# Seven block products instead of eight in the up projection of a hybrid decoder layer, with the projections around it regrouped

## The chip, the cores and the metric

The kernel runs on one core of one Trainium2 chip. Times are device microseconds (us) of one execution. The engines are PE (TensorE, matrix products; it accumulates in PSUM banks), DVE (VectorE), ACT (ScalarE), POOL (GpSimd) and SP (SyncE, which here only issues DMAs). Each engine works through its own queue in order; waits between engines go by semaphores.

## What is computed

One layer of a decoder for 576 tokens: 512 tokens of one prompt and 64 of samples (8 sequences of 8). A mixing part (a pooling branch, a recurrent branch and an attention over memory, joined by gates) gives `merged`; the change begins behind it. Of the reference that is:

```python
h = h + merged @ lw['w_out']                                   # 1024 -> 1024
xn2 = rmsnorm(h, lw['g_ffn'])
gv = xn2 @ lw['w_up']                                          # 1024 -> 2 x 3072
g_pre, val = gv[..., :D_FF], gv[..., D_FF:]
g_conv, new_ffn = causal_dwconv(g_pre, ffn_buf, lw['ffn_conv_w'], lw['ffn_conv_b'])   # 3 taps along the tokens
h = h + (jax.nn.gelu(g_conv) * val) @ lw['w_down']             # 3072 -> 1024
```

Behind it stand a last norm and the output. All is float32.

## The kernel before

Activations lie transposed: 128 features on the partitions, the 576 tokens along a row. A matrix product of float32 is made as three products of a shorter float type: weights and activations are split into a high part `wh`, `xh` (a cast on ACT, L97) and a low part `wl`, `xl` (the rest, a subtraction on DVE, L98), and PE does wh·xh, wh·xl and wl·xh for each 128 features of the inner dimension (`mm3`, L175; `wmm`, L191). A product of one 128-wide output tile with 1024 inner features is 3 x 8 x 2 = 48 matmuls, two token halves of 288 columns (`H288`) each into a PSUM bank of its own; the gate half of the up projection cuts 256 + 320 instead.

Weights stream. A class `Weights` (L113) loads each 128x1024 tile (512 KB) by a DMA on SP's queue into one of two raw buffers, two tiles ahead, and splits it into one of three pairs of high and low buffers.

Stages behind the mixing part, in the order of the program:

- `op_msplit(m)` splits the eight tiles of `merged`. The last tile is summed last (L491, DVE) after the last branch product.
- `op_out(m)` (L725), m = 0 to 7: 48 matmuls, residual add (L728), split of the normed-to-be tile, squares for the norm.
- `op_rstd_h` (L739): the sum of squares through PE (L225), a square root and Newton steps on ACT and DVE (`rs_`, `rt_`, `rv_`), and back over all partitions through PE (L249). The first tile's product is issued ahead of it.
- For each of 24 tiles j of the 3072: `op_up_g_mm`/`op_up_g` (gate: evacuation times the norm L271/L274, state copy L752, convolution L755/L757, gelu L761/L762, the value's norm L763 on POOL) and `op_up_v_mm`/`op_up_v` (value: product L774 and its split). After each eight tiles, `op_down(gr, m)` (L777) multiplies these eight into all eight output tiles; the third group runs as `op_down_last(c, m)` (L784) in token halves 320 and 256 with the last norm between (`op_fin_cols`, `op_final`, L820) and the stores (L821).

The order of issue is written out by hand (a string `MIX` and a rule in `make_schedule`); a scheduler then orders each engine's queue by it.

## Time and profile before

| | us |
|---|---|
| median of 3 runs | 975.23 (974.44 to 977.73) |
| profiled execution, its span | 974.6 |
| mixing part, up to the first product of the output projection | 447.1 |
| output projection | 51.2 |
| one tile j of the up projection | 12.8 |
| one group of `op_down` | 51.2 |

The profile gives for each engine its busy time and share of the span, the clock that was granted to TensorE, and the chain of work that ended last. The chain in order of time lists, from the end of the program back to its start, the work that released what came next; a long block of one engine without others between means that this engine set the time there. Windows give each engine's busy time in a stretch; groups by line give the mean duration of one instruction of a shape.

### The profile page before, as it was taken

How to read it: one execution, taken by the hardware profiler on the slowest of the kernel's cores; microseconds unless marked ns; L12 is line 12 of the kernel's file. 1: busy time of each engine (PE TensorE's matmuls, PEld its weight loads, DVE VectorE, ACT ScalarE, POOL GpSimd, SP SyncE). 2: the span in 40 equal slices, each digit the busy share in tenths (PEclk: the TensorE clock that was granted, in tenths of full speed). 3: DMA queues.
4: the chain of work that ended last, by engine and by line, in shares of the span. 5: the costliest groups of instructions: out<-in, count | busy, mean ns of one | idle time of the engine just before them, and what ended most of it. 6: DMA issues, size and time to landing. Idle time of an engine off the chain costs nothing.

```text
span 974.6 us, 17085 instructions
## 1 busy us (share of the span) xinstructions
PE 954.4 (98%) x7196; PEld 940.9 (97%) x7196; DVE 534.9 (55%) x768; ACT 389.3 (40%) x579; POOL 198.8 (20%) x265
## 2 busy tenths in 40 slices
...
PEclk9999999999999999999999999999999999999998
...
GB/s 227 136 77 66 77 72 70 102 159 113 77 108 131 150 198 149 142 109 88 87 87 65 87 87 88 84 69 87 87 87 85 71 84 87 87 86 71 132 156 118
DMA packets 33612, 101.00 MB, mean 104 GB/s; under 512 B 3936, under 2 KB 8032, under 8 KB 33536
## 3 DMA queue, kind: packets, MB, share of 16 engines
...
q8 instruction: 56, 0.92, 0.4%
q10 hardware_dynamic: 1088, 1.18, 0.3%
...
## 4 chain that ended last, share of the span: by engine, by line
PE 92%; DVE 4%; DMA 2%; ACT 1%; issue 1%; SPq 0%; POOL 0%; DVEq 0%; ACTq 0%
PE ps_up_g_mm L183 16%; PE ps_up_v_mm L183 16%; PE ps_gate L183 14%; PE ps_down L183 11%; PE ps_branch L183 10%; PE pq_down_last L183 5%; PE ps_out L183 5%; PE ps_rnn_mm L183 3%; PE ps_q L183 3%; PE ps_pool_mm L183 2%; PE pq_rnn_gate L183 1%; PE pq_k_mm L183 1%; PE ps_v L542 1%; DMA cv_spv<-in_cv 1%; DMA wr_start<-in_w_gate 1%
## 5 line engine op out<-in xcount | busy, mean ns | idle before, releaser
L183 PE MATMUL ps_up_g_mm<-y_out,wh_up_g_mm 128*128 128x256 f32 (+1 forms) x672 | 117.3, 297 | 0.0
L183 PE MATMUL ps_up_v_mm<-y_out,wh_up_v_mm 128*128 128x288 f32 x672 | 116.8, 296 | 0.0
L183 PEld LDWEIGHTS ps_up_g_mm<-y_out,wh_up_g_mm 128*128 128x128 f32 x672 | 101.3, 190 | 0.1
L183 PEld LDWEIGHTS ps_up_v_mm<-y_out,wh_up_v_mm 128*128 128x128 f32 x672 | 99.1, 189 | 0.0
L752 POOL COPY so_ffn<-e_up_g_mm 128x18 f32<-128x18 f32 x24 | 28.4, 1182 | 262.3 <-DVE e_up_g_mm L274 262.3
L183 PE MATMUL ps_up_g_mm<-y_out,wl_up_g_mm 128*128 128x256 f32 x336 | 72.2, 297 | 0.0
L183 PE MATMUL ps_up_v_mm<-y_out,wl_up_v_mm 128*128 128x288 f32 x336 | 72.0, 296 | 0.0
L97 ACT ACTIVATE wh_up_v_mm<-wr_up_v_mm 128x1024 fp32r<-128x1024 f32 x24 | 25.5, 1061 | 103.9 <-PE ps_up_g_mm L183 96.6
L183 PE MATMUL ps_down<-x_up_v,wh_down 128*128 128x288 f32 x384 | 66.7, 296 | 0.0
L271 DVE TENSOR_TENSOR e_up_g_mm<-ps_up_g_mm,s_rstd_h 128x512 f32<-128x512 f32 x24 | 16.6, 692 | 81.1 <-PE ps_up_g_mm L183 78.6
L183 PE MATMUL ps_gate<-x_start,wh_gate 128*128 128x288 f32 x320 | 57.0, 298 | 0.0
L183 PEld LDWEIGHTS ps_up_g_mm<-y_out,wl_up_g_mm 128*128 128x128 f32 x336 | 56.7, 190 | 0.0
L183 PEld LDWEIGHTS ps_down<-x_up_v,wh_down 128*128 128x128 f32 x384 | 56.5, 189 | 0.0
L183 PEld LDWEIGHTS ps_up_v_mm<-y_out,wl_up_v_mm 128*128 128x128 f32 x336 | 54.1, 189 | 0.0
L780 DVE TENSOR_TENSOR h<-ps_down,h 128x576 f32<-128x576 f32 x16 | 12.1, 757 | 68.0 <-PE ps_down L183 68.0
L183 PEld LDWEIGHTS ps_gate<-x_start,wh_gate 128*128 128x128 f32 x320 | 47.2, 189 | 1.0 <-issue 1.0
L761 ACT ACTIVATE g_up_g<-e_up_g 128x512 f32<-128x512 f32 x24 | 15.2, 634 | 80.2 <-DVE e_up_g L757 80.2
L97 ACT ACTIVATE wh_branch<-wr_branch 128x1024 fp32r<-128x1024 f32 (+1 forms) x24 | 22.0, 917 | 63.1 <-PE ps_gate L183 28.1
L774 DVE TENSOR_TENSOR g_up_g<-ps_up_v_mm,g_up_g 128x576 f32<-128x576 f32 x24 | 18.1, 756 | 52.6 <-POOL g_up_g L763 52.6
L97 ACT ACTIVATE wh_down<-wr_down 128x1024 fp32r<-128x1024 f32 x16 | 16.9, 1059 | 74.8 <-PE ps_down L183 72.7
L763 POOL TENSOR_TENSOR g_up_g<-g_up_g,s_rstd_h 128x576 f32<-128x576 f32 x24 | 34.6, 1443 | 58.9 <-ACT g_up_g L762 58.9
L183 PE MATMUL pq_down_last<-x_up_v,wh_down_last 128*128 128x256 f32 (+1 forms) x224 | 44.6, 295 | 0.1
...
## 6 DMA issues: line engine op xcount, KB each, us to landing
wr_up_g_mm<-in_w_up SPq DMA_DIRECT2D x21, 512.0 KB, 3.4
wr_up_v_mm<-in_w_up SPq DMA_DIRECT2D x21, 512.0 KB, 3.4
wr_down_last<-in_w_down SPq DMA_DIRECT2D x14, 512.0 KB, 3.5
wr_down<-in_w_down SPq DMA_DIRECT2D x12, 512.0 KB, 3.4
wr_gate<-in_w_gate SPq DMA_DIRECT2D x10, 512.0 KB, 3.5
ck_sscore<-in_ck SPq DMA_DIRECT2D x8, 512.0 KB, 4.4
cv_spv<-in_cv SPq DMA_DIRECT2D x8, 512.0 KB, 4.7
wr_branch<-in_w_gate SPq DMA_DIRECT2D x6, 512.0 KB, 3.7
```

The costliest lines, as they stand in the source:

```text
L97: nc.scalar.activation(hi, src, AF.Copy)
L183: nc.tensor.matmul(out[:, c, : hs.stop - hs.start], a[:, ks], b[:, hs], start=(first and k == 0 and i == 0), stop=(last and k == K - 1 and ...
L271: nc.vector.tensor_tensor(v2(ext[:, off : off + NP_]), p_[:, :, :256], v2(rbt[:, :NP_]), ALU.mult)
L542: nc.tensor.matmul(vps[:, mt, :], a[:, ms], b[:, ws], start=(k == 0 and i == 0), stop=(k == 7 and i == 2))
L752: nc.gpsimd.tensor_copy(so_ffn[:, j], sview(ext, 512, 10, 9)[:, :, 0:2])
L761: nc.scalar.activation(ge[:, :NP_], gc[:, :NP_], AF.Gelu_apprx_tanh)
L763: eng(OPT["gemul"]).tensor_tensor(ge, ge, rf, ALU.mult)
L774: nc.vector.tensor_tensor(v2(ge), p_[:, :, :TH], v2(ge), ALU.mult)
L780: nc.vector.tensor_tensor(v2(h[m]), p_[:, :, :TH], v2(h[m]), ALU.add)
```

## The change

The two factors of the up projection are cut in two: the 1024 inner features into halves K1 and K2 (four 128-wide tiles each), the output tiles of one j into gate and value, the tokens into two halves of 288. That makes a 2x2 block product, with 8 block products of 12 matmuls of 288 columns. The new code forms sums and differences of blocks and needs seven (Strassen's scheme in Winograd's form): `P1` to `P7`, 84 matmuls for a tile pair j where there were 96.

With it come:

- The normed activations are wanted in seven operand forms: `B11`, `B21`, `B22` (three of the four quarters), `T1`, `T2`, `T3`, `T4` (sums and differences). Each is made once, 1152 columns wide (four tiles of 288), by DVE additions, an ACT cast and a DVE subtraction.
- The norm is now applied to the activations themselves, in token halves (`norm`, L836), so the sum of squares is done once per token half, and the output projection runs in two token passes (`out_mm`, 24 matmuls of 288 columns for each half and tile). Five of the eight weight tiles of w_out stay in buffers between the passes (`wo_load`).
- The weight blocks are combined for each j: `R` holds two blocks and a third (768 KB, two DMAs of SP), `S` is the sum of two blocks; the second is added by a DMA that POOL issues (`accum_op`, L856). DVE adds two more (L873, L887). Five splits follow: two of 1024 columns (`prep_A`, `prep_S`) and three of 512.
- Products are combined behind PE: two PSUM banks take two block products each, three partial sums go through SBUF (`u`, `u3`, `v`): copies on ACT (L913, L919), sums on DVE (L925, L931, L941/L942, L950, L968). The first tap of the convolution moves to ACT (L957), the product with the value to POOL (L974).
- `w_down` works in six groups of four tiles; from j = 4 on, two output tiles of the group before (24 matmuls each) follow each j. The last group runs as before in columns 320 and 256 (`last_mm`, 12 matmuls), from weights kept in the form buffers. The first norm's multiplies (`final(0)`) now stand before the last product of the second columns.
- The first four j run ahead without down products: `P1` and `P2` of j = 0 to 3 stand in front, between the forms, and each of these j then has `P6`, `P7`, `P5`, `P4`, `P3`.

Matmuls from the output projection on: before 384 + 2304 + 1152 = 3840, after 384 + 2016 + 1152 = 3552.

```diff
     def op_msplit(m):
-        S["mg", m] = split(merged[m], T, tx)
-
...
+        for c, tag in enumerate(("xa", "xb")):
+            if (c, m // 2) not in mgh:
+                mgh[c, m // 2] = xu(tag, [2, 2, TH])
+            t = mgh[c, m // 2][:, m % 2]
+            split_to(t[:, 0], t[:, 1], merged[m][:, H288[c]])
...
+        def out_mm(c, m):
+            p_ = bank()
+            wh, wl = wo[m]
             for k in range(8):
...
+                x = mgh[c, k // 2][:, k % 2]
+                ks = slice(k * P, (k + 1) * P)
+                for i, (a, b) in enumerate(((wh, 0), (wh, 1), (wl, 0))):
+                    nc.tensor.matmul(
+                        p_[:, :TH], a[:, ks], x[:, b], start=(k == 0 and i == 0), stop=(k == 7 and i == 2)
+                    )
+            return p_
...
+        def out_post(c, m, p_):
+            hs = h[m][:, H288[c]]
+            nc.vector.tensor_tensor(hs, p_[:, :TH], hs, ALU.add)
+            s = tu()
+            nc.scalar.activation(s, hs, AF.Square)
...
+            nc.scalar.activation(hw[c][m // 4][:, m % 4, :], hs, AF.Identity, scale=pc(C_GFFN + m))
...
+        def load_R(j):
+            R[j] = fr.tile([P, 1536], F32, tag="R", name=nm("R"))
+            nc.sync.dma_start(R[j][:, 512:], w2(wu[j][:, 2:4]))
+            nc.sync.dma_start(R[j][:, :512], wu[j][:, 0])
+
+        def load_S(j):
+            SR[j] = raw()
+            nc.sync.dma_start(SR[j], w2(wu[j][:, 0:2]))
+            nc.gpsimd.dma_start(SR[j], w2(wu[j][:, 1:3]), accum_op=ALU.add)
...
+        def prep_A(j):
+            WA[j] = ring()
+            r = R.pop(("A", j)) if ("A", j) in R else R[j][:, 512:]
+            split_to(*WA[j], r)
+
+        def prep_S2(j):
+            r = R[j]
+            nc.vector.tensor_tensor(r[:, 512:1024], r[:, 512:1024], SR[j][:, :512], ALU.add)
+            W1[j, 6] = single()
+            split_to(*W1[j, 6], r[:, 512:1024])
+
+        def prep_S(j):
+            WS[j] = ring()
+            split_to(*WS[j], SR[j])
+
+        def prep_22(j):
+            W1[j, 4] = single()
+            split_to(*W1[j, 4], R[j][:, :512])
+
+        def prep_S4(j):
+            r = R[j]
+            nc.vector.tensor_tensor(r[:, 1024:], r[:, 1024:], r[:, 512:1024], ALU.add)
+            W1[j, 3] = single()
+            split_to(*W1[j, 3], r[:, 1024:])
...
+        def prod(p_, w, c0, x, first=True):
+            wh, wl = w
+            xh, xl = B[x]
+            for k in range(4):
+                ks = slice(c0 + k * P, c0 + (k + 1) * P)
+                for i, (a, b) in enumerate(((wh, xh), (wh, xl), (wl, xh))):
+                    nc.tensor.matmul(
+                        p_[:, :TH], a[:, ks], b[:, k, :],
+                        start=(first and k == 0 and i == 0), stop=(k == 3 and i == 2),
+                        skip_group_check=not first,
+                    )
+
+        C = {}
...
+        def P1(j):
+            C["b1", j] = bank()
+            prod(C["b1", j], WA[j], 0, "B11")
+            C["u", j] = tu()
+            nc.scalar.activation(C["u", j], C["b1", j][:, :TH], AF.Copy)
+
+        def P2(j):
+            p_ = C.pop(("b1", j))
+            prod(p_, WA.pop(j), 512, "B21", first=False)
+            C["v", j] = te(T)
+            nc.scalar.activation(C["v", j][:, :TH], p_[:, :TH], AF.Copy)
+
+        def P6(j):
+            p_ = bank()
+            prod(p_, W1.pop((j, 6)), 0, "T2")
+            u = C["u", j]
+            nc.vector.tensor_tensor(u, p_[:, :TH], u, ALU.subtract)
+
+        def P7(j):
+            C["b7", j] = p_ = bank()
+            prod(p_, WS[j], 512, "T3")
+            C["u3", j] = tu()
+            nc.vector.tensor_tensor(C["u3", j], p_[:, :TH], C["u", j], ALU.add)
+
+        def P5(j):
+            C["b5", j] = p_ = bank()
+            prod(p_, WS.pop(j), 0, "T1")
+            u3 = C.pop(("u3", j))
+            C["x", j] = ext = FF["x"].tile([P, UW], F32, tag="x", name=nm("ext"))
...
+        def P4(j):
+            p_ = C.pop(("b7", j))
+            prod(p_, W1.pop((j, 4)), 0, "T4", first=False)
+            ext = C["x", j]
+            nc.vector.tensor_tensor(ext[:, 2 : 2 + TH], p_[:, :TH], C["u", j], ALU.add)
...
+        def conv(j):
+            ext = C["x", j]
...
+            nc.scalar.activation(gc[:, :592], ext[:, 0:592], AF.Identity, scale=pc(cw), bias=pc(C_FCB + j))
+            for q_ in range(1, 3):
+                nc.vector.scalar_tensor_tensor(
+                    gc[:, :592], ext[:, q_ : q_ + 592], pc(cw + q_), gc[:, :592], ALU.mult, ALU.add
+                )
+            nc.scalar.activation(ext[:, :NP_], gc[:, :NP_], AF.Gelu_apprx_tanh)
+            nc.scalar.activation(sview(ext, NP_, 8), sview(gc, 512, 10)[:, :, 2:10], AF.Gelu_apprx_tanh)
...
+        def P3(j):
+            p_ = C.pop(("b5", j))
+            prod(p_, W1.pop((j, 3)), 0, "B22", first=False)
+            nc.vector.tensor_tensor(C["v", j][:, TH:], p_[:, :TH], C.pop(("u", j)), ALU.subtract)
+
+        prods = {}
+
+        def post(j):
+            v, ext = C.pop(("v", j)), C.pop(("x", j))
+            nc.gpsimd.tensor_tensor(v, v, ext[:, :T], ALU.mult)
+            t = xu(("xa", "xb")[j % 2], [2, T])
+            prods[j] = t[:, 0], t[:, 1]
+            split_to(t[:, 0], t[:, 1], v)
...
+        P1(0)
+        r2 = rstd_cols(sqs[1], TH)
+        P1(1)
+        prep_A(3)
+        rl2 = bcast(r2)
+        norm(1, 0, rl2)
+        norm(1, 1, rl2)
+        P2(0)
+        x11, x21 = hw[0]
+        x12, x22 = hw[1]
+        nc.vector.tensor_tensor(x11, x11, x12, ALU.subtract)
+        xt2 = xu("xa", [4, TH], F32)
+        nc.vector.tensor_tensor(xt2, x22, x11, ALU.add)
+        form("T2", 0, xt2)
+        P2(1)
+        nc.vector.tensor_tensor(x12, x12, x22, ALU.subtract)
+        prep_S(0)
+        load_S(1)
+        form("T3", 1, x12)
+        P1(2)
+        form("T1", 2, x11)
+        P1(3)
+        nc.vector.tensor_tensor(x21, x21, xt2, ALU.subtract)
+        prep_22(0)
+        form("T4", 3, x21)
+        P2(2)
+        form("B22", 4, x22)
+        prep_S4(0)
+        load_R(2)
+        P2(3)
+        hrs.close()
+        FF["x"] = pool("fx", 4)
+
...
+            n = j + 1
+            more = n < NFF
+            npre = n < NPRE
+            if not pre:
+                P1(j)
+                if more:
+                    prep_A(n)
+            P6(j)
+            if more and pre and not npre:
+                prep_A(n)
+            if more:
+                prep_S2(n)
+            if not pre:
+                P2(j)
+            P7(j)
+            P5(j)
+            if more:
+                prep_S(n)
+                if n + 1 < NFF:
+                    load_S(n + 1)
+            P4(j)
+            conv(j)
+            if more:
+                prep_22(n)
+            P3(j)
+            if more:
+                prep_S4(n)
+                if n + 2 < NFF:
+                    load_R(n + 2)
+            post(j)
+            if not pre:
+                down(g, 2 * q)
+            if more and not npre:
+                load_D(n // NFB - 1, n % NFB)
+                prep_D(n // NFB - 1, n % NFB)
+            if not pre:
+                down(g, 2 * q + 1)
...
+    def up_blocks(w):
+        b = w.reshape(2, 4, P, 2, NFF, P).transpose(4, 2, 3, 0, 1, 5)
+        return C(np.stack([b[:, :, 0, 1], b[:, :, 0, 0], b[:, :, 1, 0], b[:, :, 1, 1]], 2).reshape(NFF, P, 4, 512))
```

How the queues of DVE change is seen at three places. The first is the end of the mixing part, from the split of the last branch weight to the first residual add. Before:

```order
L98 TENSOR_TENSOR wl_branch_7_4973<-wr_branch_7_4970,wh_branch_7_4972 128x1024
L98 TENSOR_TENSOR x_msplit_5019<-g_gate_4_1487,x_msplit_5018 128x576
L487 TENSOR_TENSOR y_gate_7_4929<-ps_branch_7_4976,y_gate_7_4929 128x576
L98 TENSOR_TENSOR wl_out_5030<-wr_out_5027,wh_out_5029 128x1024
L491 TENSOR_TENSOR g_gate_7_1848<-g_gate_7_1848,y_gate_7_4929 128x576
L98 TENSOR_TENSOR x_msplit_5024<-g_gate_7_1848,x_msplit_5023 128x576
L728 TENSOR_TENSOR h<-ps_out_5033,h 128x576
```

After (`xa`, `xb` are the two token halves of a split merged tile):

```order
L112 TENSOR_TENSOR wl_branch_7_4975<-wr_branch_7_4972,wh_branch_7_4974 128x1024
L112 TENSOR_TENSOR xa_msplit_5016<-g_gate_4_1485,xa_msplit_5016 128x288
L112 TENSOR_TENSOR xb_msplit_5019<-g_gate_4_1485,xb_msplit_5019 128x288
L502 TENSOR_TENSOR y_gate_7_4929<-ps_branch_7_4978,y_gate_7_4929 128x576
L112 TENSOR_TENSOR wl_ffn<-wr_ffn,wh_ffn 128x1024
L506 TENSOR_TENSOR g_gate_7_1846<-g_gate_7_1846,y_gate_7_4929 128x576
L112 TENSOR_TENSOR xa_msplit_5009<-g_gate_7_1846,xa_msplit_5009 128x288
L112 TENSOR_TENSOR xb_msplit_5012<-g_gate_7_1846,xb_msplit_5012 128x288
L813 TENSOR_TENSOR h<-pb_ffn,h 128x288
```

The last merged tile (`g_gate_7`) is still summed behind the split of a weight; its own split is now two operations of 288, and the first residual add has 288 columns.

The second place is the start of the up stage. Before, DVE has there the norm's small operations, two weight splits and the first evacuations:

```order
L98 TENSOR_TENSOR wl_up_v_mm_5591<-wr_up_v_mm_5588,wh_up_v_mm_5590 128x1024
L229 TENSOR_SCALAR rv_rstd_h<-pq_rstd_h 128x4
L232 TENSOR_SCALAR rv_rstd_h<-pq_rstd_h 64x1
L98 TENSOR_TENSOR wl_up_g_mm_5692<-wr_up_g_mm_5689,wh_up_g_mm_5691 128x1024
L234 RECIPROCAL rs_rstd_h<-rt_rstd_h 128x8
L235 TENSOR_TENSOR rt_rstd_h<-rs_rstd_h 128x8
L236 SCALAR_TENSOR_TENSOR rt_rstd_h<-rt_rstd_h,rv_rstd_h 128x8
L237 SCALAR_TENSOR_TENSOR rs_rstd_h<-rt_rstd_h,rs_rstd_h 128x8
L271 TENSOR_TENSOR e_up_g_mm_5530<-ps_up_g_mm_5539,s_rstd_h 128x512
L274 TENSOR_TENSOR e_up_g_mm_5530<-ps_up_g_mm_5539,s_rstd_h 128x8x8
L755 TENSOR_SCALAR e_up_g_5673<-e_up_g_mm_5530,par 128x592
L757 SCALAR_TENSOR_TENSOR e_up_g_5673<-e_up_g_mm_5530,par,e_up_g_5673 128x592 x2
```

After, from the second norm half on (`hr`, `xa`: normed quarters; `b_...`: form buffers; `pd`: the norm broadcast in PSUM):

```order
L836 TENSOR_TENSOR xa_ffn<-xa_ffn,pd_ffn 128x1152 x2
L112 TENSOR_TENSOR wl_ffn<-wr_ffn,wh_ffn 128x1024
L1032 TENSOR_TENSOR hr_ffn<-hr_ffn,xa_ffn 128x1152
L112 TENSOR_TENSOR b_792_ffn<-xa_ffn,b_791_ffn 128x1152
L1034 TENSOR_TENSOR xa_ffn<-xa_ffn,hr_ffn 128x1152
L1037 TENSOR_TENSOR xa_ffn<-xa_ffn 128x1152
L112 TENSOR_TENSOR b_773_ffn<-xa_ffn,b_772_ffn 128x1152
L112 TENSOR_TENSOR wl_ffn<-wr_ffn,wh_ffn 128x1024
L112 TENSOR_TENSOR b_779_ffn<-xa_ffn,b_778_ffn 128x1152
L112 TENSOR_TENSOR b_783_ffn<-hr_ffn,b_782_ffn 128x1152
L1044 TENSOR_TENSOR hr_ffn<-hr_ffn,xa_ffn 128x1152
L925 TENSOR_TENSOR u_ffn<-pb_ffn,u_ffn 128x288
```

Between the norm and the first evacuation of a block product (L925) stand now eleven operations of 1152 columns, counting the last form's split three rows further down, and two weight splits of 1024.

The third place is one tile of the steady part. Before, one j (here the fourth):

```order
L774 TENSOR_TENSOR g_up_g_6009<-ps_up_v_mm_6019,g_up_g_6009 128x576
L98 TENSOR_TENSOR wl_up_g_mm_6079<-wr_up_g_mm_6076,wh_up_g_mm_6078 128x1024
L98 TENSOR_TENSOR x_up_v_6070<-g_up_g_6009,x_up_v_6069 128x576
L271 TENSOR_TENSOR e_up_g_mm_6073<-ps_up_g_mm_6082,s_rstd_h 128x512
L274 TENSOR_TENSOR e_up_g_mm_6073<-ps_up_g_mm_6082,s_rstd_h 128x8x8
L98 TENSOR_TENSOR wl_up_v_mm_6145<-wr_up_v_mm_6142,wh_up_v_mm_6144 128x1024
L755 TENSOR_SCALAR e_up_g_6134<-e_up_g_mm_6073,par 128x592
L757 SCALAR_TENSOR_TENSOR e_up_g_6134<-e_up_g_mm_6073,par,e_up_g_6134 128x592 x2
```

After, the part of a tile pair from the evacuation of P6 to that of P3 (`wl<-R` is the split for the next tile's P1 and P2, `wl<-wr` that of the sum `S`):

```order
L925 TENSOR_TENSOR u_ffn<-pb_ffn,u_ffn 128x288
L112 TENSOR_TENSOR wl_ffn<-R_ffn,wh_ffn 128x1024
L931 TENSOR_TENSOR u_ffn<-pb_ffn,u_ffn 128x288
L873 TENSOR_TENSOR R_ffn<-R_ffn,wr_ffn 128x512
L887 TENSOR_TENSOR R_ffn<-R_ffn 128x512
L941 TENSOR_TENSOR ext_ffn<-u_ffn,pb_ffn 128x224
L942 TENSOR_TENSOR ext_ffn<-u_ffn,pb_ffn 128x8x8
L112 TENSOR_TENSOR wl_ffn<-wr_ffn,wh_ffn 128x1024
L112 TENSOR_TENSOR sl_ffn<-R_ffn,sh_ffn 128x512
L950 TENSOR_TENSOR ext_ffn<-pb_ffn,u_ffn 128x288
L112 TENSOR_TENSOR sl_ffn<-R_ffn,sh_ffn 128x512
L968 TENSOR_TENSOR v_ffn<-pb_ffn,u_ffn 128x288
```

The split of the next tile's first weight block, the evacuation `u3` and the additions for the next tile's weights stand in that order ahead of the two evacuations L941/L942.

## Rows read from the trace of the kernel before

**Rows 1.** The page of the profile: span, PE's busy time, the granted clock in 40 slices (tenths of full speed), and the chain's shares by engine.

```profile
span 974.6 us, 17085 instructions
...
PE 954.4 (98%) x7196; PEld 940.9 (97%) x7196; DVE 534.9 (55%) x768; ACT 389.3 (40%) x579; POOL 198.8 (20%) x265
...
PEclk9999999999999999999999999999999999999998
...
PE 92%; DVE 4%; DMA 2%; ACT 1%; issue 1%; SPq 0%; POOL 0%; DVEq 0%; ACTq 0%
```

**Rows 2.** The chain that ended last in order of time: start, us, engine, what it writes, line, count of matmuls.

```profile
447.12 51.20 PE ps_out L183 x384
498.32 6.40 PE ps_up_g_mm L183 x48
...
603.36 51.20 PE ps_down L183 x384
...
910.56 33.92 PE pq_down_last L183 x240
```

**Rows 3.** Windows of core 0: stretch, its length, then busy time (and count) of PE, PE's weight loads, DVE, ACT, POOL, then the granted clock as a share, the share of time of the DMA engines, GB/s.

```profile
447.12:498.32 51.20, 51.20 (x386) 51.20 (x386) 27.07 (x33) 18.33 (x24) 0.24 (x1) 1.00 0.29 93
...
511.12:526.56 15.44, 15.44 (x117) 15.22 (x118) 10.98 (x19) 5.86 (x11) 4.40 (x9) 1.00 0.19 69
526.56:603.36 76.80, 76.80 (x578) 76.80 (x578) 42.08 (x55) 22.05 (x32) 20.01 (x25) 1.00 0.26 83
944.48:974.60 30.12, 21.57 (x174) 20.72 (x173) 15.05 (x30) 11.88 (x21) 7.33 (x6) 0.89 0.39 131
```

**Rows 4.** DVE's instructions grouped by line and shape: names, shapes, count, busy us, mean ns of one, idle time before them.

```profile
L757 DVE SCALAR_TENSOR_TENSOR e_up_g<-e_up_g_mm,par,e_up_g 128x592 f32<-128x592 f32 x48 | 41.1, 857 | 1.7
L98 DVE TENSOR_TENSOR wl_up_v_mm<-wr_up_v_mm,wh_up_v_mm 128x1024 fp32r<-128x1024 f32 x24 | 29.4, 1226 | 3.9 <-ACT wh_up_v_mm L97 3.8
...
L98 DVE TENSOR_TENSOR x_up_v<-g_up_g,x_up_v 128x576 fp32r<-128x576 f32 x24 | 18.8, 784 | 0.8 <-ACT x_up_v L97 0.8
...
L780 DVE TENSOR_TENSOR h<-ps_down,h 128x576 f32<-128x576 f32 x16 | 12.1, 757 | 68.0 <-PE ps_down L183 68.0
L274 DVE TENSOR_TENSOR e_up_g_mm<-ps_up_g_mm,s_rstd_h 128x64 f32<-128x64 f32 x24 | 5.2, 215 | 0.0
L792 DVE TENSOR_TENSOR h<-pq_down_last,h 128x320 f32<-128x320 f32 x8 | 3.9, 492 | 10.2 <-PE pq_down_last L183 10.2
L792 DVE TENSOR_TENSOR h<-pq_down_last,h 128x256 f32<-128x256 f32 x8 | 3.4, 425 | 6.6 <-PE pq_down_last L183 6.5
...
L98 DVE TENSOR_TENSOR wl_branch<-wr_branch,wh_branch 128x512 fp32r<-128x512 f32 x5 | 3.4, 682 | 0.0
```

**Rows 5.** The same view for ACT.

```profile
L97 ACT ACTIVATE wh_up_v_mm<-wr_up_v_mm 128x1024 fp32r<-128x1024 f32 x24 | 25.5, 1061 | 103.9 <-PE ps_up_g_mm L183 96.6 <-issue 7.3
...
L97 ACT ACTIVATE x_up_v<-g_up_g 128x576 fp32r<-128x576 f32 x24 | 16.4, 685 | 7.6 <-DVE g_up_g L774 7.6
L761 ACT ACTIVATE g_up_g<-e_up_g 128x512 f32<-128x512 f32 x24 | 15.2, 634 | 80.2 <-DVE e_up_g L757 80.2
...
L762 ACT ACTIVATE g_up_g<-e_up_g 128x64 f32<-128x64 f32 x24 | 5.8, 241 | 0.0
```

**Rows 6.** The same view for POOL.

```profile
L763 POOL TENSOR_TENSOR g_up_g<-g_up_g,s_rstd_h 128x576 f32<-128x576 f32 x24 | 34.6, 1443 | 58.9 <-ACT g_up_g L762 58.9
L752 POOL COPY so_ffn<-e_up_g_mm 128x18 f32<-128x18 f32 x24 | 28.4, 1182 | 262.3 <-DVE e_up_g_mm L274 262.3
L745 POOL COPY e_up_g_mm<-st_ffn 128x16 f32<-128x16 f32 x23 | 11.9, 518 | 0.0
```

**Rows 7.** The timeline at the end of the mixing part: start, us, engine, line, operation, names and shapes.

```profile
444.79 1.43 POOL L491 TENSOR_TENSOR g_gate<-g_gate,y_gate 128x576 f32<-128x576 f32 x1 [7.79 <-DVE y_gate L487]
444.94 2.36 DVE L98 TENSOR_TENSOR wl_branch<-wr_branch,wh_branch 128x1024 fp32r<-128x1024 f32 x1 [0.23 <-ACT wh_branch L97]
...
448.56 1.21 DVE L98 TENSOR_TENSOR wl_out<-wr_out,wh_out 128x1024 fp32r<-128x1024 f32 x1
...
449.69 0.74 DVE L491 TENSOR_TENSOR g_gate<-g_gate,y_gate 128x576 f32<-128x576 f32 x1
...
450.47 0.69 ACT L97 ACTIVATE x_msplit<-g_gate 128x576 fp32r<-128x576 f32 x1 [2.52 <-DVE g_gate L491]
...
451.19 0.76 DVE L98 TENSOR_TENSOR x_msplit<-g_gate,x_msplit 128x576 fp32r<-128x576 f32 x1 [0.75 <-ACT x_msplit L97]
```

**Rows 8.** The chain in order of time around the sum of squares.

```profile
511.12 0.99 PE pq_rstd_h L225 x10
512.11 2.99 PE ps_up_g_mm L183 x21
515.10 1.25 PE pq_rstd_h L249 x10
```

**Rows 9.** The end of the program: the chain in order of time, and from the timeline the multiplies of the first norm half.

```profile
958.09 3.08 PE pq_down_last L183 x24
...
961.29 3.11 PE pq_down_last L183 x24
...
958.13 3.01 DVE L820 TENSOR_TENSOR h<-h,pq_final 128x640 f32<-128x640 f32 x4 [0.38 <-PE pq_final L814]
```

**Rows 10.** DMA issues: what is written from what, issuing queue, count, KB of one, median us from issue to landing.

```profile
wr_up_g_mm<-in_w_up SPq DMA_DIRECT2D x21, 512.0 KB, 3.4
...
o_k<-e_k POOLq DMA_DIRECT2D x2, 256.0 KB, 2.9
...
o_ffn<-so_ffn POOLq DMA_DIRECT2D x1, 216.0 KB, 4.1
```

360 lines of the change are left out of this document (230 added, 130 removed), and 3 rows, old and new, of the table OPS.

## The prediction

> **What bounds the kernel now.** First the page: PE is busy 98% of the span at a granted clock that is full (2.4 GHz) in all slices but the last, and the chain that ended last is 92% PE [rows 1]. Then the chain in order of time: from the output projection to the last down projection it is PE blocks end to end with no other engine between them, but for one sum of squares [rows 2]. Then the windows: in the output projection and in the tiles of the up stage PE is busy for all of the stretch, DVE for about half, ACT and POOL less [rows 3]. So here time is the number of matmuls times the time of one: 48 matmuls of 288 columns take 6.40 us, 51.20/384 gives the same 133.3 ns [rows 2]. It is the same when all matmuls of a product go into one PSUM bank, as the new block products do: the last down group does that and takes 33.92 us for 192 matmuls of 320 columns and 48 of 256; with 288 columns at 133.3 ns and the extra columns at 1/2.4 ns, these come to 192 x 146.7 + 48 x 120 = 33.9 us [rows 2].
>
> **The change part by part.** Its sum is made against the profiled 974.6 us [rows 1]; the median shown is 975.23, 0.6 more, and I add that at the end.
>
> (a) *Matmuls.* Out 384 before and after, up 24 x 96 = 2304 before and 24 x 84 = 2016 after, down 1152 both. 288 fewer x 133.3 ns = **-38.4 us**. The mixing part before the output projection has the same instructions; only their order changes, in its first 100 us. I cost that at 0, with 2 us either way.
>
> (b) *First pass of the output projection.* Before, the first product used the last merged tile after 42 of its 48 matmuls; now after 21 of 24, 2.8 us after 447.12, at 449.9. That tile's chain was: sum 449.69, cast 450.47, low part 451.19 to 451.95 [rows 7]. With half the width in the last two steps it ends at about 451.4 to 451.9, and nothing else can run on PE. **+2.0** (1.5 to 2.3).
>
> (c) *Two sums of squares instead of one.* Before: 0.99 + 1.25 us of PE, and 15.44 - 12.80 = 2.64 us in all between first and second tile [rows 3, 8]. Now two half-wide ones, as much PE work. The first one's scalar chain (3.0 us from the end of one PE piece to the start of the other [rows 8]) lies beside second-pass products. The second has only one block product, 1.6 us, over it: 1.4 us are bare. 2.2 + 1.4 - 2.64 = **+1.0** (0 to 2).
>
> (d) *Head of the up stage.* This is the only stretch where DVE, not PE, sets the end. From the second broadcast of the norm on, DVE has in order 11 operations on 1152 columns and two weight splits of 1024 before the fourth operand form is done. 1152 columns are not in the trace: 512 take 682 ns and 1024 take 1226 [rows 4], so 1.06 ns a column and 1.36 us. 11 x 1.36 + 2 x 1.23 = 17.4 us. Then each tile pair j = 0 to 3 costs DVE 9.6: four evacuations of 288 at 0.46 (between 425 ns at 256 columns and 492 at 320), the 224-column and 8x8 ones at 0.39 and 0.22, a 1024 split 1.23, five 512-wide operations at 0.68, two conv steps at 0.86, one 576 split 0.78 [rows 4]. The first pair has no 576 split yet (8.8), the third has one more 1024 split, of the fourth only what stands before its last product counts (4.9): 17.4 + 8.8 + 9.6 + 10.8 + 4.9 = 51.5 us. PE has in the same stretch 25 block products, 40.0 us. The difference is 11.5. Successive independent DVE operations start some 0.07 us before the end of the one before (the two of 448.56 and 449.69: 1.13 apart at a duration of 1.21 [rows 7]), over 60 operations up to 4 less. But one operation in it waits for more than DVE: the second tile's summed weight block can be loaded only when DVE's split of the first has given its buffer back, and DVE asks for the sum three 1152-column operations and one evacuation, 4.5 us, later. The load takes 3.4 us and the adding DMA of (g) at least the 2.9 of the nearest store [rows 10], so some 2 to 7 us are bare, behind which all of DVE's queue stands. I take 11.5 - 4 + 4.5 = **+12** (6 to 20). No down projection and no first block product stands in these tiles to cover it: that is what is late next once the matmuls are gone.
>
> (e) *Tiles j = 5 to 23.* Each has 132 matmuls, 17.6 us of PE. DVE's sum is 13.6 us: 9.6 as above, two residual adds of 757 ns and two more splits of 1024 [rows 4]. ACT's is about 8.3 (three casts of 1.06, one of 0.69, three of 512 at about 0.6, copies, the first conv step, gelu 0.63 + 0.24 [rows 5]), POOL's about 4 [rows 6]. None is full, so only the order counts. The tightest edge starts at the end of the second product, which gives back the weight slot: cast 1.06, split 1.23, u3 0.46, two 512 adds 0.68 each, the two evacuations 0.39 + 0.22 that read the bank in which the last of the seven products accumulates: 4.7 us, while PE has three products, 4.8, before that one. It just fits, with hand-overs of hundredths between ACT and DVE. I take 0.1 a tile, **+2** (0 to 8). POOL's own operations come behind the fourth product's evacuation, so not in these 4.7 us.
>
> (f) *Tail.* The order changes: the first norm's four multiplies (3.01 us on DVE [rows 9]) now stand one product of 12 matmuls ahead of the end instead of two of 24 (3.08 + 3.11 us [rows 9]): the last residual add waits about 1.6. Last group's first product waits for the last tile's split, +0.5. **+2.1** (0 to 4).
>
> (g) *Accumulating DMA.* The sum of two weight blocks is made by a second DMA that POOL issues and that adds in SBUF. No such DMA is in the trace. Nearest: 512 KB loads 3.4 us, POOL-issued stores of 216 to 256 KB 2.9 to 4.1 us [rows 10]. In the steady tiles it stands in a loop: DVE's split of one tile's sum gives the buffer back, the load follows (3.4), the adding DMA, then DVE's two 512 adds, two evacuations and the split of the next tile's sum (0.68 + 0.68 + 0.39 + 0.22 + 1.23 = 3.2). With half a us of hand-overs this fits into 17.6 us while the DMA takes up to 10.5. DMA engines are busy 26% there [rows 3] and rise with the bytes (2.25 MB for 17.6 us, 128 GB/s against 83). I take 3 to 8 us, the upper end twice the slowest row, as it reads and writes its target. That is inside the cover: cost 0 outside of (d).
>
> Sum: -38.4 + 2.0 + 1.0 + 12 + 2 + 2.1 = -19.3; 974.6 - 19.3 = 955.3, with the 0.6 **956 us**.
>
> One thing speaks against (d). A POOL elementwise operation and a DVE one met once near the end of the mixing part: POOL's add began 444.79, DVE's split 444.94 took 2.36 us instead of 1.23 [rows 7, 4]. The Trainium skill (SBUF — State Buffer, Who interferes with whom) says that a DVE instruction with two SBUF inputs contends with a GpSimd instruction that reads SBUF, and that the second is fully blocked. The trace agrees (2.36 against 1.23). By this rule the sum is R2's 965, without it 956.
>
> **Rivals.**
> R1, *only the count matters.* DVE's head is hidden: its operations overlap more, or the forms are ready ahead of need. For it: DVE is at half load in all these windows [rows 3]. Against it: an in-order queue with 51.5 us of work beside 40. It gives (d) and (e) 0: 974.6 - 38.4 + 2 + 1 + 2.1 + 0.6 = **942**.
>
> R2, *POOL slows DVE where DVE is the bound.* Almost all new DVE operations read two SBUF tiles, and POOL does per tile one multiply of 1.44 us and copies of 0.52 and 1.18 [rows 6]. Two meetings a tile at 1.13 us (2.36 against 1.23), over four tiles of the head, are +9; in the later tiles DVE has 4 us to spare. **965**. Against it: many head operations read PSUM, and POOL has 4 us of work a tile.
>
> R3, *the accumulating DMA is the bound* (slower). If it takes longer than 10.5 us, the 512-wide add that needs its result stands at the head of DVE's queue, and behind it every evacuation that frees a PSUM bank: PE stops in each tile, one us for each us over, 19 times. At 11.5 us the gain of 19 is eaten; at three times the slowest row, 12.3, it is 956 + 1.8 x 19 = **990**. For it: no row shows an adding DMA, and its reading of the target is extra traffic. Against it: rows of 3 to 4 us.
>
> **How the numbers follow.** Forecast 0.60, own range 947 to 964 ((d) from 6 to 18, (e) from 0 to 4, mixing part 2 either way, not all at one end); R1 0.13; R2 0.19; R3 0.08. 0.3% is 2.9 us, about what can be told here from no change; all but R3 is faster than that: 0.92. R3 ends within it only for a DMA of 11.3 to 11.6 us: same 0.01, slower 0.07. The range 941 to 970 takes in R1 and R2, with (d) at its upper end.
>
> **What would show it.** Right: from j = 5 on the tile pairs follow each other at 17.6 to 17.7 us with PE over 98% busy and 133 ns a matmul; between the second norm broadcast and the fourth tile's last product a stretch of 50 to 60 us with PE at 70 to 80%, DVE over 80%, and one DVE wait of some us for a DMA on the second tile's sum. Wrong: a wait of PE for DVE evacuations in every later tile ((e) too small, and the release of the weight slot is the place); there a DVE wait for a DMA (R3); DVE splits of 1024 columns at over 2 us in the head (R2); a head with PE full (R1). A lower granted clock behind the head's idle times would break it too: in the last 30 us of before, with PE idle in 28% of them, 0.89 was granted [rows 3].

## The result and the profile after

The changed kernel takes **954.51 us** (median of 4 runs, 952.03 to 955.98) against 976.29 for the kernel before, run beside it (4 runs, 974.44 to 977.73): ratio 0.978, 95% interval 0.975 to 0.980, so 2.2% faster. The profiled execution took 953.88 us with a span of 952.1, 22.5 less than the 974.6 of [rows 1].

The page of the changed kernel:

```profile
span 952.1 us, 17091 instructions
...
PE 921.6 (97%) x6924; PEld 905.3 (95%) x6924; DVE 623.2 (65%) x974; ACT 468.6 (49%) x745; POOL 222.3 (23%) x302
...
PEclk9999999999999999999999999999999999999998
...
PE 85%; DVE 8%; DMA 2%; ACT 2%; issue 2%; POOL 1%; SPq 0%; DVEq 0%; ACTq 0%; POOLq 0%
```

Against [rows 1]: PE's share of the chain falls from 92% to 85% and DVE's doubles to 8%. PE got 288 matmuls less, 38 us by their count, but is still the bound of most of the span. Where DVE entered the chain is seen in the chain in order of time (start, us, what; [rows 2] are the same view):

```profile
450.84 25.92 PE pb_ffn L806 x194
476.76 1.00 PE pd_ffn L239 x12
...
484.33 0.78 PE pd_ffn L829 x6
485.11 16.09 PE pb_ffn L806 x120
...
502.80 1.00 PE pd_ffn L239 x12
503.80 1.79 PE pb_ffn L901 x12
505.59 0.78 PE pd_ffn L829 x6
506.36 1.67 PE pb_ffn L901 x11
...
522.26 6.09 DMA wr_ffn<-in_w_up
...
535.43 2.22 POOL v_ffn L974
...
577.92 11.19 PE pb_ffn L901 x84
589.11 6.39 PE pd_ffn L987 x48
...
911.94 16.96 PE pb_ffn L1114 x120
...
938.23 3.02 DVE h L1148 x4
```

Two stretches are PE alone: the output projection from 450.84 on, and everything from 577.92, the start of the sixth tile pair (j = 5), to 911.94. Between 506.36 and 577.92 the chain goes through other engines and one DMA. I call 505.59 to 577.92, from the second norm's broadcast (L829) to the sixth tile, the *head stretch*. The windows (as in [rows 3]: length, busy time and count of PE, weight loads, DVE, ACT, POOL, then granted clock, DMA share, GB/s):

```profile
505.59:577.92 72.33, 64.48 (x452) 61.64 (x452) 65.57 (x91) 38.80 (x59) 18.07 (x28) 0.98 0.56 148
...
533.00:536.00 3.00, 0.61 (x2) 0.65 (x3) 2.99 (x6) 2.76 (x5) 0.57 (x1) 0.81 0.94 212
536.00:539.00 3.00, 3.00 (x16) 3.00 (x16) 2.80 (x3) 1.32 (x2) 1.64 (x1) 0.62 0.98 318
...
700.98:718.56 17.58, 17.58 (x135) 17.58 (x134) 12.34 (x20) 7.81 (x13) 4.03 (x5) 1.00 0.49 136
911.94:952.10 40.16, 30.02 (x223) 29.37 (x221) 15.19 (x36) 17.28 (x35) 9.70 (x12) 0.91 0.18 60
```

A steady tile (the window from 700.98) is 17.58 us, 132 matmuls at 133.2 ns, PE busy all of it. In the head stretch DVE is busy 91%, more than PE's 89%. From 506.40 to 559.39 DVE works through the forms, the first three tile pairs and the fourth up to the last evacuation (L942) ahead of that pair's last product: 53.0 us, of which it is busy 49.0.

What stops it there is read from the timeline of the same kernel (start, us, engine, line, in brackets the idle time before and what ended it):

```profile
450.33 0.46 DVE L112 TENSOR_TENSOR xa_msplit<-g_gate,xa_msplit 128x288 fp32r<-128x288 f32 x1 [0.51 <-ACT xa_msplit L111]
...
450.35 0.89 PE L806 MATMUL pb_ffn<-xa_msplit,wh_branch 128*128 128x288 f32 x2 [1.10 <-ACT xa_msplit L111]
...
522.26 0.87 POOL L856 DMA_DIRECT2D wr_ffn<-in_w_up  x1 [6.84 <-DVE u_ffn L925]
...
528.44 1.06 ACT L111 ACTIVATE wh_ffn<-wr_ffn 128x1024 fp32r<-128x1024 f32 x1 [5.00 <-DMA wr_ffn<-in_w_up]
529.40 0.61 ACT L111 ACTIVATE sh_ffn<-R_ffn 128x512 fp32r<-128x512 f32 x1
...
530.05 0.69 DVE L112 TENSOR_TENSOR sl_ffn<-R_ffn,sh_ffn 128x512 fp32r<-128x512 f32 x1 [3.19 <-ACT sh_ffn L111]
...
534.79 0.45 DVE L931 TENSOR_TENSOR u_ffn<-pb_ffn,u_ffn 128x288 f32<-128x288 f32 x1
535.15 1.22 DVE L112 TENSOR_TENSOR wl_ffn<-wr_ffn,wh_ffn 128x1024 fp32r<-128x1024 f32 x1
...
535.38 0.82 PE L901 MATMUL pb_ffn<-b_ffn,sh_ffn 128*128 128x288 f32 x2 [3.42 <-ACT ext_ffn L963]
535.43 2.21 POOL L974 TENSOR_TENSOR v_ffn<-v_ffn,ext_ffn 128x576 f32<-128x576 f32 x1 [3.93 <-ACT ext_ffn L963]
536.29 1.91 DVE L112 TENSOR_TENSOR sl_ffn<-R_ffn,sh_ffn 128x512 fp32r<-128x512 f32 x1
...
543.98 1.89 POOL L974 TENSOR_TENSOR v_ffn<-v_ffn,ext_ffn 128x576 f32<-128x576 f32 x1 [2.15 <-DVE u_ffn L925]
544.88 2.07 DVE L112 TENSOR_TENSOR wl_ffn<-wr_ffn,wh_ffn 128x1024 fp32r<-128x1024 f32 x1
...
709.90 0.22 DVE L942 TENSOR_TENSOR ext_ffn<-u_ffn,pb_ffn 128x64 f32<-128x64 f32 x1
...
710.41 0.43 PE L901 MATMUL pb_ffn<-b_ffn,sh_ffn 128*128 128x288 f32 x2
```

The first two rows belong to the output projection's start and come up under (b), the last two to a steady tile and come up under (e). Of the others the reader is to see a chain of four: the adding DMA for the third pair's sum lands 6.1 us after its issue at 522.26; ACT's cast of that sum stands first in ACT's queue and waits 5.00; the small cast behind it (sh_ffn) needs no DMA but is late with it; DVE waits 3.19 for that small cast, and with it all that stands behind it in DVE's queue; PE then waits 3.42. The bracket at PE's row names the gelu L963, which ended at about the same time. But the product that begins there (P4 of the second pair) needs no gelu: it adds to the bank that the evacuation L931 reads until 535.24. In the version without POOL's multiplies below, PE's wait at the same place is put down to L931. After that wait TensorE's matmuls come at about 0.24 us each until 538.2: the granted clock is 0.81 and 0.62 in the two windows from 533, so the lower level, 1.2 GHz, was granted in part of them. The rows from 535.15 to 544.88 show DVE and POOL meeting, splits of 1.91 and 2.07 us beside a POOL multiply.

Grouped by line and shape, and the DMA issues:

```profile
L974 POOL TENSOR_TENSOR v_ffn<-v_ffn,ext_ffn 128x576 f32<-128x576 f32 x24 | 36.2, 1510 | 101.1 <-ACT ext_ffn L963 97.5
L112 DVE TENSOR_TENSOR wl_ffn<-wr_ffn,wh_ffn 128x1024 fp32r<-128x1024 f32 x47 | 59.0, 1255 | 0.3 <-ACT wh_ffn L111 0.2
...
L112 DVE TENSOR_TENSOR sl_ffn<-R_ffn,sh_ffn 128x512 fp32r<-128x512 f32 x72 | 50.8, 707 | 4.2 <-ACT sh_ffn L111 4.2
```

```profile
wr_ffn<-in_w_up SPq DMA_DIRECT2D x17, 512.0 KB, 3.7
wr_ffn<-in_w_up POOLq DMA_DIRECT2D x17, 512.0 KB, 6.2
```

The second pair is from the steady tiles: a plain load lands 3.7 us after its issue, an adding DMA 6.2.

**Where the 22.5 us are.** Output projection's start (its first matmul) to the last group's start is 446.27 to 911.94, 465.7 us; before it was 446.96 to 910.56, 463.6. In between 96 matmuls are gone (-12.8), so 14.9 us were added. The last group on takes 40.16 instead of 64.04 us: 192 matmuls less (-25.6) and 1.7 more. The start is 0.7 earlier, which is less than it wanders (see the experiments). So -38.4 - 0.7 + 14.9 + 1.7 = -22.5. The 14.9 come out in the trace as follows. From 446.27 to the end of the first pass and one product of the second, 476.76, are 30.5 us for 216 matmuls of 133.2 ns: 1.7 more than these. From there to 506.36, behind the second broadcast, 192 matmuls leave 4.0, against 2.64 in the kernel before: 1.4. From 506.36 to 577.92, 444 matmuls leave 12.4. From there to 911.94, 19 tiles of 132 matmuls leave nothing. That is 15.5; the 0.6 over 14.9 are time that the kernel before had beyond its matmuls at 133.2 and its 2.64.

### The profile page after: what moved, and what is told of

Same layout as the page of the kernel before. It is cut to its first block, busy times and chain, and to the rows that moved or that the text cites. A ratio compares the mean times of both kernels' runs of the same rounds, so it can differ in the third digit from the quotient of the medians.

```text
span 952.1 us, 17091 instructions
## 1 busy us (share of the span) xinstructions
PE 921.6 (97%) x6924; PEld 905.3 (95%) x6924; DVE 623.2 (65%) x974; ACT 468.6 (49%) x745; POOL 222.3 (23%) x302
## 4 chain that ended last, share of the span: by engine, by line
PE 85%; DVE 8%; DMA 2%; ACT 2%; issue 2%; POOL 1%; SPq 0%; DVEq 0%; ACTq 0%; POOLq 0%
PE pb_ffn L901 24%; PE ps_gate L197 15%; PE pd_ffn L987 13%; PE ps_branch L197 10%; PE pb_ffn L806 5%; PE ps_rnn_mm L197 3%; PE ps_q L197 3%; PE pb_ffn L1114 3%; PE ps_pool_mm L197 2%; PE pq_rnn_gate L197 1%; PE pq_k_mm L197 1%; PE ps_v L557 1%; DVE wl_ffn L112 1%; DMA wr_start<-in_w_gate 1%; DMA wr_ffn<-in_w_up 1%
## 5 line engine op out<-in xcount | busy, mean ns | idle before, releaser
L901 PE MATMUL pb_ffn<-b_ffn,wh_ffn 128*128 128x288 f32 x768 | 155.5, 296 | 1.0 <-ACT b_ffn L111 0.5
L901 PE MATMUL pb_ffn<-b_ffn,sh_ffn 128*128 128x288 f32 x576 | 118.8, 299 | 6.9 <-ACT ext_ffn L963 3.4
L901 PEld LDWEIGHTS pb_ffn<-b_ffn,wh_ffn 128*128 128x128 f32 x768 | 123.4, 188 | 1.5 <-ACT b_ffn L111 0.7
L901 PE MATMUL pb_ffn<-b_ffn,wl_ffn 128*128 128x288 f32 x384 | 113.1, 295 | 0.0
L901 PEld LDWEIGHTS pb_ffn<-b_ffn,sh_ffn 128*128 128x128 f32 x576 | 93.2, 190 | 8.8 <-ACT ext_ffn L963 3.6
L901 PE MATMUL pb_ffn<-b_ffn,sl_ffn 128*128 128x288 f32 x288 | 85.1, 297 | 0.0
L901 PEld LDWEIGHTS pb_ffn<-b_ffn,wl_ffn 128*128 128x128 f32 x384 | 72.3, 188 | 0.0
L974 POOL TENSOR_TENSOR v_ffn<-v_ffn,ext_ffn 128x576 f32<-128x576 f32 x24 | 36.2, 1510 | 101.1 <-ACT ext_ffn L963 97.5
L112 DVE TENSOR_TENSOR wl_ffn<-wr_ffn,wh_ffn 128x1024 fp32r<-128x1024 f32 x47 | 59.0, 1255 | 0.3 <-ACT wh_ffn L111 0.2
L856 POOL DMA_DIRECT2D wr_ffn<-in_w_up x24 | 21.3, 889 | 159.5 <-DMA wr_ffn<-in_w_up 99.1
L987 PE MATMUL pd_ffn<-xa_ffn,wh_ffn 128*128 128x288 f32 x320 | 55.8, 296 | 0.0
L987 PE MATMUL pd_ffn<-xb_ffn,wh_ffn 128*128 128x288 f32 x320 | 55.6, 295 | 0.0
```

The costliest lines, as they stand in the source:

```text
L112: nc.vector.tensor_tensor(lo, src, f(hi), ALU.subtract)
L856: nc.gpsimd.dma_start(SR[j], w2(wu[j][:, 1:3]), accum_op=ALU.add)
L901: nc.tensor.matmul(p_[:, :TH], a[:, ks], b[:, k, :], start=(first and k == 0 and i == 0), stop=(k == 3 and i == 2), skip_group_check=not f ...
L974: nc.gpsimd.tensor_tensor(v, v, ext[:, :T], ALU.mult)
L987: nc.tensor.matmul(p_[:, c, :TH], a[:, ks], b[:, hs], start=(k == 0 and i == 0), stop=(k == NFB - 1 and i == 2),)
```

## The experiments

My theory after reading the trace: the head stretch is bound by the amount of DVE's work, with two additions to it: one stall handed on from the third pair's adding DMA through ACT's queue (3.2 us of DVE), and four meetings of DVE splits with POOL's multiplies (536.29, 544.88, 555.60 and 565.55; 1.22 + 0.85 + 0.87 + 1.24 = 4.2 us more than the same shapes alone). Rivals: the adding DMA itself is the limit, in the steady tiles too; or the order of hand-overs, not the amount, sets the stretch.

The time before the head stretch wanders by itself: its start lay between 504.6 and 508.2 us in the twelve traces of this section and the one above (that with doubled adding DMAs aside), and up to there their code is the same. Most of this is there at the output projection's first matmul, 445.3 to 448.9 us in these traces. The tail wanders too: from the last group's start to the end it takes 39.4 to 40.4 us in the traces that have its code unchanged. So single spans are not compared below 2 us; the head stretch is. Where its code is the same it repeats within 0.3 us: 72.3, 72.5 and, in the run that changes only the tail, 72.4.

**The third sum without its DMA.**

```diff
-            nc.gpsimd.dma_start(SR[j], w2(wu[j][:, 1:3]), accum_op=ALU.add)
+            if j != 2:
+                nc.gpsimd.dma_start(SR[j], w2(wu[j][:, 1:3]), accum_op=ALU.add)
```

> Leaves out the adding DMA of the third tile pair (j = 2), so its weight block is one block and not a sum. In the changed kernel that DMA was issued at 522.26, landed at 528.36, ACT's cast of the sum stood at the head of ACT's queue until 528.44, behind it ACT's next cast, and DVE idled 3.19 us before that one's low part; PE then waited 3.42 us and ran some 3 us at the lower clock. Theory A (the wait in ACT's queue is a part of the head's cost): DVE's idle time goes, and the fifth tile's last pieces and the sixth tile's start (577.9 in the changed kernel) come 3 to 4 us earlier. Rival B (the head is DVE's total work, this wait only shifts idle time that DVE has anyway): less than 1 us.

Measured 955.51 us (one run); head stretch 74.8 us, 2.5 longer. The 3.19 us wait of DVE is gone, but the orders on the engines were planned anew (at least 12 of DVE's 91 rows in the stretch stand elsewhere): DVE now waits 2.2 and 2.0 us for ACT's casts of the gated products, and 2.3 for PE, and the granted clock of the stretch is 0.95 instead of 0.98. This doesn't tell the theories apart; it shows that a wait removed in this way brings another order along. The next try kept all instructions, and with them the orders of DVE and PE.

**A buffer of its own for the third sum.** The load of that sum had to wait until a split gave back its buffer; here it gets one.

```diff
-            SR[j] = raw()
+            SR[j] = xu("xb", [1152], F32)[:, :1024] if j == 2 else raw()
```

> The third tile pair's sum is loaded into a free activation buffer of its own, so its load need not wait for DVE's split of the first sum (517.9 in the changed kernel). Result unchanged. Theory A: the sum lands before ACT asks for it, DVE's 3.19 us of idle time and PE's 3.42 us go, the sixth tile starts 3 to 4 us earlier and the kernel takes about 0.4% less. Rival B: less than 1 us, no difference in the times.

Measured 953.12 us (5 runs, 951.92 to 954.84), ratio to before 0.977 (0.975 to 0.978); head stretch 70.9 us, 1.5 shorter, more than rival B's 1 us and half of the 3 to 4 that I had expected. The wait was passed on, by the same mechanism:

```profile
528.84 1.06 ACT L111 ACTIVATE wh_ffn<-wr_ffn 128x1024 fp32r<-128x1024 f32 x1 [3.98 <-DMA wr_ffn<-in_w_up]
...
530.45 0.69 DVE L112 TENSOR_TENSOR sl_ffn<-R_ffn,sh_ffn 128x512 fp32r<-128x512 f32 x1 [2.18 <-ACT sh_ffn L111]
```

This cast is the fourth pair's, which took the place of the third's at the head of ACT's queue.

**Buffers for the third and the fourth sum.** The same line with `j in (2, 3)`.

> The third and the fourth tile pair's sums get buffers of their own. With one such buffer the wait only passed on: ACT's queue then held the fourth sum's cast in the same place, and DVE idled 2.2 us there. Result unchanged. Theory A (an adding DMA at the head of ACT's queue is a part of the head's cost): DVE's wait for that cast falls below 1 us and the sixth tile starts 2 to 4 us before 577.9. Rival B (DVE's total work and the collisions with POOL set the head, the wait shifts only where DVE idles): under 1 us.

Measured 953.99 us (one run); head stretch 70.4 us, 2.0 shorter than in the changed kernel. That small cast no longer makes DVE wait; the longest waits of DVE for ACT are now two others of 1.9 and 1.7 us. So the stall was worth 2.0 us of time, not the 3.2 us of DVE's idle time or the 3.4 of PE's. The orders of DVE and PE are those of the changed kernel. The granted clock of the stretch is 1.00 here, so the matmuls at the lower clock, some 1.3 us, are gone with the stall; how much of the 2.0 is theirs is not shown.

**No POOL multiply in the first four tile pairs.** The gate's multiplication by the other half is left out there.

```diff
-            nc.gpsimd.tensor_tensor(v, v, ext[:, :T], ALU.mult)
+            if j >= NPRE:
+                nc.gpsimd.tensor_tensor(v, v, ext[:, :T], ALU.mult)
```

> Leaves out POOL's multiply of gelu and value for the first four tile pairs, so their products are the value alone. In the changed kernel the four multiplies took 2.21, 1.89, 1.90 and 1.45 us, and beside them one DVE split each took 1.91 instead of 0.69, 2.07, 2.09 and 2.46 instead of 1.22. Theory C (POOL and DVE block each other): these four splits take 0.69 and 1.22 again, and the sixth tile starts 3 to 4 us earlier. Rival (something else, DMA traffic or the clock, slowed them): they stay near 2 us, and the start moves by less than 1 us.

Measured 952.4 us (one run). The window of the head stretch:

```profile
505.40:576.57 71.17, 63.75 (x453) 61.73 (x452) 61.63 (x91) 39.85 (x60) 12.11 (x24) 0.98 0.59 152
```

DVE's 91 instructions take 61.63 us instead of 65.57, 3.9 less, and its splits 0.69 and 1.22 again: the meetings are real and of the size read. The stretch is only 1.2 us shorter. DVE's wait behind the third sum remains (3.1 us), and it now idles 9.5 us in the stretch instead of 6.8; the longest of the other waits are 2.2 and 1.9 us for casts of ACT. A few operations also stand in another order.

**The same multiplies on DVE.**

```diff
-            nc.gpsimd.tensor_tensor(v, v, ext[:, :T], ALU.mult)
+            (nc.vector if j <= NPRE else nc.gpsimd).tensor_tensor(v, v, ext[:, :T], ALU.mult)
```

> The first five tiles' multiplies go from POOL to DVE (about 0.76 us each there); nothing else changes, so the buffer wait of the third pair stays. Measured by the stretch from the second norm's broadcast to the sixth tile's first product: 72.3 us in the changed kernel, 70.4 with two buffers more, 69.7 with both. Theory (DVE's work and ACT's wait for the sum each hold the stretch up, and either alone gives part): collisions of 4.1 us go, 3.0 us of multiplies come, so 71.3 to 72.3. Rival (the multiplies are what the combination's gain came from): 70 or less.

Measured 955.72 us (one run), head stretch 72.0 us, 0.3 shorter, no more than it wanders: what the meetings cost is about what the multiplies cost on DVE. Here too the orders were planned anew (at least 9 of the 91 rows on DVE), in the same way as in the next version.

**Both: two buffers and the multiplies on DVE.**

> The two buffers, and for the first five tile pairs the multiply of gelu and value on DVE instead of POOL. Result unchanged. Leaving that multiply out brought 4.1 us less DVE time but only 1.4 us of the start, because DVE then idled 5.3 us, 3.1 of it for the cast behind the adding DMA. Theory A + C (both count, together): DVE is as busy as before (five multiplies of 0.76 us against collisions of 4.2), the chain from gelu to split is 1.1 us shorter a tile, and the sixth tile starts 3 to 5 us earlier than 577.9; the kernel takes 0.3 to 0.5% less than the changed one. Rival B: under 1 us.

> The combined version once more. If its gain is the 2.6 us that its stretch is shorter by: 2 to 4 us under the changed kernel of the same call. If its lower time was a matter of which executions were compared: the same time within 1 us.

> The changed kernel itself, unchanged, beside the combined version on one chip: 953 to 956 us. It gives the difference to the combined version without the detour over different runs of before, and with a second trace how far the time before the up stage wanders from execution to execution.

Measured 950.42 us (5 runs, 948.55 to 952.94), ratio to before 0.974 (0.972 to 0.975). In a second series, on one chip: the combined version 950.69 (4 runs, 948.67 to 952.84), ratio 0.974 (0.972 to 0.977), the changed kernel 955.34 (5 runs, 953.78 to 956.30), ratio 0.979 (0.977 to 0.981). The two sets do not overlap: the combined version is 4.7 us faster than the changed kernel. Its head stretch is 69.7 us in the first trace and 69.4 in the second, against 72.3 and 72.5, so 2.6 to 3.1 of these are shown; the other 1.5 to 2 are not located. The sixth tile starts at 576.35, 1.6 us earlier than 577.92 and not the 3 to 5 expected: the stretch is 2.6 shorter, but began 1.1 later in that trace. Between the two buffers alone (70.4, one trace) and this version lie 0.7 to 0.9 us; whether they come from the multiplies or from the order on DVE, which is another here, is not shown.

**Less work for DVE.** In the combined version three DVE operations of each of the first four pairs are left out.

```diff
-            nc.vector.tensor_tensor(r[:, 512:1024], r[:, 512:1024], SR[j][:, :512], ALU.add)
+            if j >= NPRE:
+                nc.vector.tensor_tensor(r[:, 512:1024], r[:, 512:1024], SR[j][:, :512], ALU.add)
...
-            nc.vector.tensor_tensor(r[:, 1024:], r[:, 1024:], r[:, 512:1024], ALU.add)
+            if j >= NPRE:
+                nc.vector.tensor_tensor(r[:, 1024:], r[:, 1024:], r[:, 512:1024], ALU.add)
...
-            for q_ in range(1, 3):
+            for q_ in range(1 if j >= NPRE else 2, 3):
```

> The combined version (two buffers more, multiplies on DVE) with three DVE operations of each of the first four tiles left out: the two additions that make the sums of weight blocks (0.60 us each) and one of the convolution's two multiply-adds (0.75 us), so 4 x 1.95 = 7.8 us less DVE work and the values of those tiles wrong by what is left out. The stretch from the second norm's broadcast to the sixth tile was 69.7 us, of it some 60 us TensorE's. Theory (the amount of DVE work bounds the stretch): 5 to 8 us shorter, 62 to 65 us, TensorE then over 94% busy in it. Rival (the order in which DVE, ACT and the DMAs hand the work on bounds it, whatever the amount): under 2 us shorter, 68 us or more.

Measured 947.25 us (one run). The head stretch of the combined version and of this one:

```profile
506.67:576.35 69.68, 63.52 (x453) 61.60 (x452) 64.97 (x96) 39.41 (x60) 9.13 (x23) 0.98 0.53 136
```

```profile
507.43:571.57 64.14, 61.59 (x452) 60.12 (x452) 59.00 (x87) 39.85 (x61) 9.02 (x23) 1.00 0.60 152
```

5.5 us shorter for 7.8 us of operations left out (6.0 in busy time, since a few other operations came into the window); PE is now busy 96% of it, and the granted clock is full. The stretch went down nearly one for one with DVE's busy time, and DVE idled 5.1 us in it, where it had idled 4.7. That is what the theory of the amount says. But the run does not tell amount from order by itself: the scheduler planned the queues anew (at least 18 of the 86 DVE rows that both versions have stand elsewhere), and one of the additions left out is what waited for the adding DMA's sum on DVE. For the amount as the main part speaks that DVE is busy 91 to 93% of the stretch in the changed kernel, the combined version and this one, each with an order of its own; against the amount alone, that 3.9 us less in the run without POOL's multiplies brought 1.2.

**Each adding DMA made twice.**

```diff
+            nc.gpsimd.dma_start(SR[j], w2(wu[j][:, 1:3]), accum_op=ALU.add)
```

> Makes every adding DMA twice, one behind the other, so a weight sum takes about 6.2 + 0.9 + 6.2 us instead of 6.2. Theory A (in the tiles from j = 5 on the adding DMA is covered; by the trace it lands some 11 us before it is asked for): the tile period stays 17.58 us, PE has no wait there; only the head gets longer, by 6 to 12 us for the third tile's sum and perhaps one more. Rival R3 (the adding DMA is near being the bound): the period grows by 2 to 7 us, 40 to 130 us in all.

Measured 973.23 us (one run), 19.3 more. One window from the head stretch's start to the seventh pair's, and one steady tile after it:

```profile
511.92:615.12 103.20, 86.80 (x584) 83.51 (x584) 77.94 (x111) 47.67 (x73) 27.70 (x40) 0.93 0.67 162
...
615.12:632.70 17.58, 17.58 (x134) 17.58 (x134) 12.31 (x19) 7.82 (x13) 3.56 (x6) 1.00 0.71 172
```

The steady tile hides a second adding DMA for nothing: 17.58 us, as without. That refutes the adding DMA as the limit there. All of the loss lies before the seventh pair: 13.3 us in this window (89.9 in the changed kernel) and 6.3 before it, in the output projection and with what wanders there. That is more than I had expected of the head: from 450 to 600 ACT's weight casts wait 17.9 us in all for DMAs into these buffers.

**One block product twice in each steady tile.** The result is the same; a product of 12 matmuls is written and then written again.

```diff
+            if j >= NPRE:
+                prod(p_, W1[j, 6], 0, "T2")
```

> Does the second block product (P6) twice in each tile pair from j = 4 on; the second time starts its PSUM bank anew, so the result is unchanged. Eight products of 12 matmuls then stand there as many as before the change, with all the new work on DVE, ACT and POOL kept. Theory (PE's count is the time in these tiles): the period goes from 17.58 to 19.18 us, 12 x 133.3 ns, 20 times, 32 us in all. Rival (an edge on DVE or ACT sets the period, which only happens to be near PE's): less than 1 us a tile.

Measured 987.84 us (one run), 33.9 more in the span, of which 32.0 are 20 tiles by 12 matmuls at 133 ns:

```profile
600.59:619.77 19.18, 19.18 (x147) 19.18 (x146) 12.34 (x20) 7.81 (x13) 4.02 (x5) 1.00 0.46 124
```

17.58 + 1.60 = 19.18: in the steady tiles the number of matmuls alone is the time. Of the other 1.9 us, 1.0 is the later start of the head stretch and 0.9 that stretch itself, whose order is slightly another.

**The first norm one product earlier at the end.**

```diff
-            if m == 6:
+            if m == 5:
```

> The first norm's multiplies are issued one product of 12 matmuls earlier in the tail. In the changed kernel they ran 938.23 to 941.25, and the last residual add waited behind them 1.7 us after its product had ended. Theory (f) (that order costs the tail): the part from the last group's first product to the end goes from 40.2 us to some 38.7. Rival (the tail is set by the last norm's chain and the stores, whatever the order): no change within 0.3 us.

Measured 954.83 us (one run). From the last group's start to the end it takes 39.86 us instead of 40.16, 0.3 less and well inside the 39.4 to 40.4 of the unchanged tail: no effect is shown, and the 1.5 us expected did not come. The multiplies did start 1.4 us earlier (24.85 us after that start instead of 26.29), but now two residual adds wait behind them instead of one:

```profile
938.09 3.02 DVE L1148 TENSOR_TENSOR h<-h,pd_ffn 128x640 f32<-128x640 f32 x4 [0.38 <-PE pd_ffn L1141]
...
941.02 0.75 DVE L1119 TENSOR_TENSOR h<-pb_ffn,h 128x256 f32<-128x256 f32 x2
```

The second-last add then has a square and a POOL addition behind it, all late. A step moved forward in DVE's queue made its new follower late; my expectation had followed the last add alone.

## Why the prediction was right, and where it was not

For the span 974.6 - 19.3 = 955.3 was forecast, and 952.1 came. The 3.2 between are: steady tiles -2.0, the time before the output projection -0.7, (b) -0.3, (c) +0.4, (d) +0.4, (f) -0.4, and the 0.6 that the kernel before had over its matmuls. The terms:

- **(a) matmuls, -38.4.** Right. 133.2 ns a matmul, and the experiment with a product twice shows that a matmul costs this and no more. The mixing part's new order was costed at 0 with 2 either way. The output projection began 0.7 us earlier in this trace, but 0.3 later in a second trace of the same kernel (447.3 against 446.96 before), so no effect of that order is shown.
- **(b) first pass, +2.0.** Measured 1.7, in its range of 1.5 to 2.3. The last tile's sum came 0.6 us earlier (449.07 against 449.69 [rows 7]), but PE was 0.7 earlier too. The row at 450.35 shows both halves of the cost: 1.10 us of waiting for the cast, and two matmuls in 0.89 instead of 0.43, because the second needs the low part, which DVE writes from 450.33 to 450.79.
- **(c) two sums of squares, +1.0.** Measured 1.4, in its range of 0 to 2. The size is near by luck, since two errors of the parts nearly cancel. I had 2.2 of PE and 1.4 bare, 3.6 in all; the step that failed is "as much PE work" for two sums of half the width. PE's four pieces take 1.00 + 0.78 + 1.00 + 0.78 = 3.56 us, where the two full-width ones had taken 0.99 + 1.25 [rows 8], and only some 0.5 of the 4.0 is bare: the second norm's scalar chain, for which I had 3.0 us, takes 1.79 from 503.80 to 505.59, and the 12 matmuls in it are 1.60.
- **(d) head, +12.** Measured 12.4: the size is right, in part by parts that cancel. DVE took 53.0 us from the broadcast to the last evacuation ahead of the fourth pair's last product, where I had 51.5 - 4 + 4.5 = 52. It is busy 49.0 of these: 46.1 of plain work, where I had 47.5, and 2.9 of meetings with POOL (the fourth lies behind 559.39), where I had none. It is idle 4.0, of which 3.2 is the one wait, where I had 4.5. That the amount of work sets the end fits the run that left out 7.8 us of it and won 5.5, but is not shown by it, since the order changed too. What was wrong is the place of the wait: "the second tile's sum", in DVE's queue. It was the third's, and it stood in ACT's queue, one step ahead of the addition that I looked at. Two buffers take turns: the second pair's load went out at 510.40, and for its sum only ACT waited, 2.88 us at 519.92; the third pair's load went out at 517.99, right behind the split of the first sum (ended 517.92). For the third, DVE waited 3.2 us for a cast whose own input was ready but which stood behind that sum's cast. I had priced a load that waits for a buffer and then the adding DMA, which is what happened, but had not followed the tile's first reader, which is the cast. PE was busy about 81% by its count of matmuls (322 x 133 ns in 53.0), near the forecast 70 to 80, DVE 93%.
- **(e) steady tiles, +2.** Measured 0, the lower end of its range: PE waits for nothing from 577.92 to 911.94. The tightest edge that I read exists and just holds: in one tile (700.98 to 718.56) the last evacuation (the row at 709.90) ended at 710.12 and the product that needs its bank began at 710.41. The 0.1 us a tile that I took was not there; the step that failed is "I take 0.1 a tile".
- **(f) tail, +2.1.** Measured 1.7 in this trace; the tail's wander of 1 us is the limit of this reading. The last residual add stood behind the norm's multiplies (938.23, 3.02 us) until 941.25, where its product ended near 939.7: 1.6 us, as forecast.
- **(g) adding DMA, 3 to 8 us, covered.** 6.2 us in the steady tiles, 5.4 to 6.3 in the head. In one steady tile the load was issued at 703.54, the adding DMA at 707.80; it landed 6.6 us later, and the result was asked for at about 725.9, so some 11.5 us of cover remain, as the doubled DMA confirms.

The rivals. *Only the count matters* (942) had nothing for the head; 12.4 us were measured there, with DVE busy 91%. *The adding DMA is the bound* (990) falls in the steady tiles; in the head it is behind a stall worth 2.0 us. *POOL slows DVE* was true in kind but not in price: I had two meetings for each of four tiles at 1.13 us, +9; there was one for each, 4.2 us of DVE in all, and without them the stretch was only 1.2 us shorter. The Trainium skill (SBUF — State Buffer, Who interferes with whom) calls the shared port pair of DVE and GpSimd an exclusive lock. The trace agrees: in the four meetings the splits took 1.91 instead of 0.69 and 2.07, 2.09 and 2.46 instead of 1.22, and POOL's multiplies 2.21, 1.89, 1.90 and 1.45, where before the mean was 1.44 [rows 6]; so in three of them both engines lost time, not DVE alone, and each to what already ran. The split of 535.15 kept its 1.22 us, the multiply that began beside it at 535.43 took 2.21 and ended at 537.64, and the next split, begun at 536.29, ended 0.56 us behind that.
